# PEER expert gates: scattered into tables in DRAM and read back, in place of one-hot matmuls

## The chip, the cores and the metric

One Trainium2 chip; the kernel runs on one of its cores. The metric is device time in microseconds of one execution. Times of single executions are shown as median, lowest and highest; a profile is of one execution, whose own time is given beside it.

## The reference, cut to what matters

Two transformer layers for 256 tokens of width 2048 (a gated delta net with memory attention, then pooling and sparse attention), and at the end of the second an expert layer with 16384 experts, which the change touches:

```python
def peer_ffn(x, wq, sub_keys, u, v):          # per token, 8 heads
    qh = (xc @ wq).reshape(PEER_CHUNK, PEER_HEADS, 2, PEER_HALF)
    s1 = jnp.einsum('thd,kd->thk', qh[:, :, 0], sub_keys[0])
    s2 = jnp.einsum('thd,kd->thk', qh[:, :, 1], sub_keys[1])
    v1, i1 = lax.top_k(s1, PEER_TOPK)         # 16 of 128 first keys
    v2, i2 = lax.top_k(s2, PEER_TOPK)         # 16 of 128 second keys
    cand = v1[..., :, None] + v2[..., None, :]
    cidx = i1[..., :, None] * PEER_KEYS + i2[..., None, :]
    best, pos = lax.top_k(cand, PEER_TOPK)    # 16 of 256 pairs
    expert = jnp.take_along_axis(cidx, pos, axis=-1)
    gate = jax.nn.softmax(best, axis=-1)
    act = jax.nn.gelu(jnp.einsum('td,thkd->thk', xc, u[expert]))
    return jnp.einsum('thk,thkd->td', gate * act, v[expert])
```

An expert is a pair (i, j) of a first and a second key. Each token has 8 x 16 = 128 picks, and one expert may be picked by several heads: its gates then add.

## The kernel before

The kernel does not gather rows of u and v. It multiplies all 256 tokens with all 16384 rows of u, applies gelu, multiplies each of the 256 x 16384 results by its gate (zero for an expert that was not picked), and multiplies that by all rows of v. The results stand in `G`, a tile of 128 partitions (the second key j) x 128 rows (the first key i) x 256 tokens, 128 KB a partition.

All matrix products are made of three matmuls per tile in a rounded fp32 form (`fp32r`): weights and activations are split into a high part and a remainder. Class `Stream` (`ws`, L40 on) brings the weights of all matrices one after the other as granules of 512 KB: SP issues the load into a `wraw` tile, ACT copies the high part to `wh`, DVE subtracts it for the remainder `wl`. From w_q on there are three tiles of each. A granule of w_u feeds 24 matmuls, and w_u has 256 granules: two for each row i. `wstat` (L304) runs w_u by pairs of rows and calls `u_done` for each pair, which writes gelu of the sums into `G`. All multiplications, additions and copies below go through one helper, so most rows of the profile have its line, L123.

Side work is written as generators in a list `sides`. While PE's matmuls are emitted, `pump` steps the generators, and these hold back their next instruction until an estimated clock of their engine is near PE's (`after`, `on`, `spare`). So the program's order on each engine is fixed when it is built, and each engine's queue runs in that order.

The routing and the gates are such generators. `route()` (L1577 on) takes each head as the second half of w_q completes it: two small fp32 products per half of the tokens give the scores, DVE takes the best 16 of each side, of the 256 sums again 16, and after the last head picks the key numbers by comparisons (`eq`), softmaxes the gates and transposes both so that tokens lie along the free axis (`pickT`, `ghl`). Its scratch tiles lie in rows of `G` that w_u has not reached. `gate()` then walks over the tokens by two, 128 times:

```python
            for a in range(2):
                pe.matmul(out=ps[:, a * 256:a * 256 + 256], lhsT=oj[:, a, :],
                          rhs=og2[:, a].rearrange("p h i -> p (h i)"), start=True, stop=True)
            if t0:
                into(t0 - 2)
```

`oj` is the one-hot form of a token's 128 second keys (128 picks x 128 keys), `og2` that of its first keys times the gates, high part and remainder; the product is the token's 128 x 128 table of gates. DVE builds the one-hots (`oi`, `oj`), ACT scales them (`og2`, four instructions), and `into` adds the two parts and multiplies them into the rows of `G` that hold gelus already. `u_done` does the converse for tokens whose gates stand there.

After w_u, `split_h` splits the rows of `G` in turn for the product with w_v, into four tile pairs (`eog`, `eghl`, `eoj`, `ewg`). During w_v, `residual()` loads `hres` and `row` on POOL's queue and applies the last norm's terms on DVE.

Of the kernel before, what the change touches and what calls it, by code (L numbers as in the profile page):

```python
# [23 lines left out]
T = 256  # L24
# [14 lines left out]
class Stream:  # L39


    def __init__(self, nc, act, dve, pool, granules, raw_bufs, split_bufs):
        self.nc, self.act, self.dve, self.src = nc, act, dve, granules
        self.nl = self.ns = self.ng = 0
        self.raw, self.parts = {}, {}
        self.raw_slots = [(pool, f"wraw{n}") for n in range(raw_bufs)]
        self.split_slots = [(pool, f"{n}") for n in range(split_bufs)]
        self.extra, self.until = [], 0

# [13 lines left out]
    def _load(self):  # L63
        if self.nl < len(self.src):
# [6 lines left out]
            self.nl += 1  # L71

# [81 lines left out]
def tile_blocks(ctx, tc, P, out, dbg=None, stop=None):  # L154
# [1022 lines left out]
    cap[0] = 4  # L1177
    for k in range(2):
        split_y(16 + k, (yh[:, k, :], yl[:, k, :]))
    for c in range(4):  # L1180
        if c > 1:
            pts[c % 2] = [bank(), bank()]
            out_mm(c, 0, 16, hh, hl)
# [9 lines left out]
    if stop == "x1":  # L1193
        return

# [341 lines left out]
    pickT = rp.tile([128, 2, T], BF16, name="pickT")  # L1537
    iof = odd[:, :32].bitcast(U8)
    pool.iota(iof, pattern=[[1, 128]], base=0, channel_multiplier=0, allow_small_or_imprecise_dtypes=True)
# [21 lines left out]
    eq = carve(92, [128, 16])  # L1561
    idf = carve(90, [2, 8, 2, 16])
    pab = carve(88, [2, 2, 128])
    pk = carve(84, [2, 3, 128])
    sk = carve(83, [2, 128])
    act.dma_start(out=sk, in_=P["sk"])
    st4 = {"q": 0, "t0": 0, "ib": 0}
# [15 lines left out]
    def route():  # L1583
        for h in range(8):
# [12 lines left out]
            for t in range(2):  # L1597
# [5 lines left out]
                yield from spare("V", SV)  # L1603

        dve.tensor_copy(out=idf, in_=idxs)
        sm = odd[:, 32:].rearrange("p (t h) -> p t h", t=2)
        for t in range(2):
            tt(pk[:, t, 2, :].rearrange("p (h r) -> p h r", h=8), best[:, t], bc(best[:, t, :, 0:1], [128, 8, 16]), OP.subtract)
        act.activation(out=pk[:, :, 2, :], in_=pk[:, :, 2, :], func=AF.Exp)
        pf = pos.rearrange("p t h r -> p t (h r)")  # L1610
        ts(pab[:, 1].bitcast(U32), pf, 15, None, op0=OP.bitwise_and)
        ts(pf, pf, 4, None, op0=OP.logical_shift_right)
        dve.tensor_copy(out=pab[:, 0], in_=pf)
        yield
        dve.reduce_sum(out=sm, in_=pk[:, :, 2, :].rearrange("p t (h r) -> p t h r", h=8), axis=AX.X)
        dve.reciprocal(out=sm, in_=sm)
        dve.tensor_copy(out=pab[:, 1], in_=pab[:, 1].bitcast(U32))
        for t in range(2):
            g = pk[:, t, 2, :].rearrange("p (h r) -> p h r", h=8)
            tt(g, g, bc(sm[:, t, :, None], [128, 8, 16]), OP.mult)  # L1620
        yield
        eq4 = eq.rearrange("p (h r) a -> p h r a", h=8)
        for t in range(2):
            for f in range(2):
                tt(eq, bc(iof[:, None, :16], [128, 128, 16]), bc(pab[:, f, t, :, None], [128, 128, 16]), OP.is_equal)
                yield from spare("V", SV)
                tt(eq4, eq4, bc(idf[:, t, :, f, None, :], [128, 8, 16, 16]), OP.mult)
                yield from spare("V", SV)
                dve.reduce_sum(out=pk[:, t, f, :], in_=eq, axis=AX.X)
                yield from spare("V", SV)  # L1630
        for t in range(2):
            ps = yield from get()
            for j in range(3):
                pe.transpose(out=ps[:, j * 128:j * 128 + 128], in_=pk[:, t, j, :], identity=ident)
            yield
            sl = slice(t * 128, t * 128 + 128)
            copy_act(pickT[:, :, sl], ps[:, :256].rearrange("p (j t) -> p j t", j=2))
            copy_act(ghl[:, 0, sl], ps[:, 256:384])
            dve.follow("A")
            tt(ghl[:, 1, sl], ps[:, 256:384], ghl[:, 0, sl].bitcast(F32), OP.subtract)  # L1640
            put(ps)
        yield
        sides.append(gate())

    def gate():

        st4["on"] = True
        ohs, sums = {}, {}

        def one_hots(t0):  # L1650
            oi = rp.tile([128, 2, 128], BF16, name="oi", bufs=2)
            oj = rp.tile([128, 2, 128], F32R, name="oj", bufs=2)
            sl = slice(t0, t0 + 2)
            tt(oi, bc(iof[:, None, :], [128, 2, 128]), bc(pickT[:, 0, sl, None], [128, 2, 128]), OP.is_equal)
            tt(oj, bc(iof[:, None, :], [128, 2, 128]), bc(pickT[:, 1, sl, None], [128, 2, 128]), OP.is_equal)
            ohs[t0] = oi, oj

        def gated(t0):
            og2 = rp.tile([128, 2, 2, 128], F32R, name="og2")
            for a in range(2):  # L1660
                for p in range(2):
                    act.activation(out=og2[:, a, p, :], in_=ohs[t0][0][:, a, :], func=AF.Copy,
                                   scale=ghl[:, p, t0 + a:t0 + a + 1].bitcast(F32))
            ohs[t0] += (og2,)

        def into(t0):
            ps, w, wg = sums.pop(t0)
            ib = st4["ib"]
            sl = slice(t0, t0 + 2)
            if ib < 128:  # L1670
                tt(G[:, ib:, sl], wg[:, ib:], w[:, 1, ib:], OP.add)
            if ib:
                tt(wg[:, :ib], wg[:, :ib], w[:, 1, :ib], OP.add)
                tt(G[:, :ib, sl], G[:, :ib, sl], wg[:, :ib], OP.mult)
            put(ps)
            st4["t0"] = t0 + 2

        one_hots(0)
        one_hots(2)
        yield from on("V")  # L1680
        gated(0)
        ready = clk["A"], clk["V"]
        for t0 in range(0, T, 2):
            while clk["P"] < max(ready) - 0.4:
                yield
            t = clk["P"]
            ps = yield from get()
            _, oj, og2 = ohs.pop(t0)
            for a in range(2):
                pe.matmul(out=ps[:, a * 256:a * 256 + 256], lhsT=oj[:, a, :],  # L1690
                          rhs=og2[:, a].rearrange("p h i -> p (h i)"), start=True, stop=True)
            if t0:
                into(t0 - 2)
            yield from on()
            w = ps.rearrange("p (t h i) -> p h i t", t=2, h=2)
            wg = rp.tile([128, 128, 2], F32, name="wg", bufs=2)
            if t0 + 2 < T:
                gated(t0 + 2)
                ra = clk["A"]
            copy_act(wg, w[:, 0])  # L1700
            sums[t0] = ps, w, wg
            if t0 + 4 < T:
                one_hots(t0 + 4)
            ready = ra, clk["V"]
            while clk["P"] < t + TICK:
                yield
        into(T - 2)
        split_h(0)
        split_h(1)

    HS = {}
# [16 lines left out]
    def u_done(c0, m, pt):  # L1728
        t0 = st4["t0"]
# [267 lines left out]
```

## Time and profile before

| what | value |
|---|---|
| time, median of 3 runs | 2809.67 us (2805.61 to 2814.22) |
| the profiled execution's own time | 2811.53 us |
| its span, first to last instruction | 2809.8 us |
| granted clock of TensorE, mean | 0.996 |
| weights from DRAM | 490.27 MB on the first hardware queue |
| instructions of PE | 19455 matmuls |
| instructions of DVE, ACT, POOL | 3530, 2626, 595 |

Busy time of an engine is the time in which it executes; its share is over the whole span and averages over stages with different limits. PE is a busy engine here, so the table by stretch and the chain of waits say where something other than PE sets the pace.

### The profile page before, as it was taken

To read this page: it belongs to the slowest core of one execution; us is meant where nothing else is said; L and a number is where in the kernel's file an instruction comes from. 1 tells how busy PE (TensorE), PEld (TensorE's weight loads), DVE (VectorE), ACT (ScalarE), POOL (GpSimd) and SP (SyncE) were. 2 spreads that over 40 slices of the span, in tenths; PEclk is the share of its full clock that TensorE was granted. 3 is DMA by queue.
4 is the path that set the end of the run, shared out by engine and by line. 5 is a ranking of instruction groups with operands and counts; after the bars stand their busy time and mean duration, and the time that the engine had idled before them with its cause. 6 is when DMAs were issued, how large, how long until landed. Compare 5 with 4: busy or idle time off the path is not lost.

```text
span 2809.8 us, 50244 instructions
## 1 busy us (share of the span) xinstructions
PE 2774.0 (99%) x19455; PEld 2554.2 (91%) x19455; DVE 1907.1 (68%) x3530; ACT 1569.4 (56%) x2626; POOL 281.0 (10%) x595
## 2 busy tenths in 40 slices
PE   9999999999999999999999999999999999999998
PEld 7999999999888999879999999999998888888886
DVE  5746777775554655657998777778876655665555
ACT  7455666665544444444445777777765555445553
POOL 0001655654001000000000000000010000000000
PEclk9999999999999999999999999999999999999999
DMA  8636655555566666446666566666666766666664
GB/s 301 182 120 185 198 167 176 167 166 171 183 190 183 190 199 183 146 149 204 189 186 190 178 181 181 181 181 181 181 213 216 221 192 193 193 195 194 193 192 140
DMA packets 147839, 522.17 MB, mean 186 GB/s; under 512 B 18848, under 2 KB 20440, under 8 KB 147088
## 3 DMA queue, kind: packets, MB, share of 16 engines
q1 hardware_dynamic: 135504, 490.27, 57.6%
q0 software_dynamic: 8272, 19.43, 2.7%
q10 hardware_dynamic: 3824, 9.26, 0.9%
q8 instruction: 152, 2.49, 0.4%
q14 instruction: 87, 0.71, 0.1%
HBM read 512.84 MB, written 5.99 MB: 185 GB/s over the span
## 4 chain that ended last, share of the span: by engine, by line
PE 94%; DVE 2%; DMA 2%; ACT 1%; issue 1%; SPq 0%; POOL 0%; ACTq 0%; POOLq 0%; DVEq 0%
PE bank L123 94%; DMA wrawwraw<-in_w_v 1%; DVE wl L123 1%; ACT wh L123 0%; DVE hres L123 0%; DMA wrawx<-in_w_kv 0%; DMA wrawwraw<-in_w_q 0%; DVE small L123 0%; ACT y L123 0%; DMA G<-in_sk 0%; DMA hot<-in_bucket_hot 0%; ACT whx L123 0%; DVE sso L123 0%; DVE wlx L123 0%; DVE wko L123 0%
## 5 line engine op out<-in xcount | busy, mean ns | idle before, releaser
L123 DVE TENSOR_TENSOR wl<-wrawwraw,wh 128x1024 fp32r<-128x1024 f32 (+1 forms) x837 | 1020.4, 1224 | 688.5 <-ACT wh L123 686.4
L123 ACT ACTIVATE wh<-wrawwraw 128x1024 fp32r<-128x1024 f32 (+1 forms) x837 | 882.1, 1058 | 865.4 <-PE bank L123 732.2
L123 PE MATMUL bank<-hh,wh 128*128 128x256 f32 x3376 | 949.0, 281 | 1.1 <-ACT hh L123 1.1
L123 PE MATMUL bank<-hl,wh 128*128 128x256 f32 x3376 | 941.0, 279 | 0.4 <-DVE hl L123 0.2
L123 PE MATMUL bank<-hh,wl 128*128 128x256 f32 x3376 | 940.1, 278 | 0.0
L123 PEld LDWEIGHTS bank<-hh,wh 128*128 128x128 f32 x3376 | 638.3, 189 | 2.5 <-ACT hh L123 1.4
L123 PEld LDWEIGHTS bank<-hl,wh 128*128 128x128 f32 x3376 | 637.0, 189 | 1.3 <-DVE hl L123 0.9
L123 PEld LDWEIGHTS bank<-hh,wl 128*128 128x128 f32 x3376 | 634.8, 188 | 0.0
L123 ACT ACTIVATE og<-oi,ghl 128x128 fp32r<-128x128 bf16 x512 | 162.9, 390 | 25.7 <-PE bank L123 25.1
L123 DVE TENSOR_TENSOR wlx<-wrawx,whx 128x1024 fp32r<-128x1024 f32 x96 | 118.1, 1230 | 82.7 <-ACT whx L123 82.6
L123 ACT ACTIVATE whx<-wrawx 128x1024 fp32r<-128x1024 f32 x96 | 101.8, 1060 | 122.3 <-PE bank L123 112.5
L123 PE MATMUL bank<-wh,eghl 128*128 128x512 f32 x512 | 147.5, 389 | 0.6 <-ACT wh L123 0.6
L123 PE MATMUL bank<-wh,eog 128*128 128x512 f32 x512 | 147.4, 389 | 0.0
L123 PE MATMUL bank<-wh,ewg 128*128 128x512 f32 x512 | 147.4, 389 | 0.0
L123 PE MATMUL bank<-wh,eoj 128*128 128x512 f32 x512 | 147.4, 389 | 0.0
L123 PEld LDWEIGHTS bank<-wh,eghl 128*128 128x128 f32 x512 | 96.0, 188 | 20.9 <-ACT wh L123 1.0
L123 PEld LDWEIGHTS bank<-wh,eog 128*128 128x128 f32 x512 | 96.0, 188 | 20.3 <-ACT wh L123 0.4
L123 PEld LDWEIGHTS bank<-wh,ewg 128*128 128x128 f32 x512 | 96.2, 188 | 19.9
L123 PEld LDWEIGHTS bank<-wh,eoj 128*128 128x128 f32 x512 | 96.1, 188 | 19.8
L123 PE MATMUL bank<-gh,wh 128*128 128x256 f32 x392 | 110.6, 282 | 0.0
L123 PE MATMUL bank<-gl,wh 128*128 128x256 f32 x392 | 108.5, 277 | 0.0
L123 PE MATMUL bank<-gh,wl 128*128 128x256 f32 x392 | 108.4, 277 | 0.0
(394 smaller groups left out, 4540.4 us busy)
## 6 DMA issues: line engine op xcount, KB each, us to landing
wrawwraw<-in_w_u SPq DMA_DIRECT2D x256, 512.0 KB, 3.8
wrawwraw<-in_w_v SPq DMA_DIRECT2D x256, 512.0 KB, 4.3
wrawwraw<-in_w_dn SPq DMA_DIRECT2D x134, 512.0 KB, 4.3
wrawwraw<-in_w_out SPq DMA_DIRECT2D x73, 512.0 KB, 3.6
wrawwraw<-in_w_in SPq DMA_DIRECT2D x61, 512.0 KB, 4.2
wrawx<-in_w_dn SPq DMA_DIRECT2D x44, 512.0 KB, 3.7
wrawwraw<-in_w_q SPq DMA_DIRECT2D x32, 512.0 KB, 4.2
wrawwraw<-in_w_kv SPq DMA_DIRECT2D x23, 512.0 KB, 5.7
```

The lines of the kernel that those rows point to most:

```text
L123: return f(*a, **kw)
```

## The change

The gates of all experts are built in two tables in DRAM (`W_d`, one for each half of the tokens, [j, i, token], 8 MB each). The tables are filled with zeros by 64 transfers of 256 KB out of a tile that POOL clears; SP issues one behind each weight load, 32 in w_out and 32 in w_in2. `route()` computes picks and softmax per head (`gates_of`), adds up the gates of repeated picks by 32 DVE instructions that compare a pick's code with all picks so far and accumulate the products, and POOL writes each of the 16 x 2 columns of 128 sums to its 128 places by an indirect transfer, so the last write of a repeated pick has the full sum. `gating()` loads the tables by pairs of rows i, from w_u's row 92 on, and DVE multiplies `G` by them. `u_done` is only the gelu. The one-hot work, the transposes, and `gate()` go.

```diff
@@ class Stream
+        self.between, self.gap = iter(()), 0
@@ def _load
                 self.nc.sync.dma_start(out=t[:, sl], in_=self.src[self.nl][:, sl])
             self.raw[self.nl] = t
             self.nl += 1
+            self.gap -= 1
+            if self.gap < 0:
+                for o, i in self.between:
+                    self.nc.sync.dma_start(out=o, in_=i)
+                    break
@@ before w_out
+    W_d = [dram.tile([128, 128, 128], F32, name=f"W_d{t}") for t in range(2)]
+    zsrc = y_t[:, 24:, :].rearrange("p a t -> p (a t)")
+    zeros = [(W_d[t][:, 4 * n:4 * n + 4, :], zsrc[:, 512 * (n % 4):512 * (n % 4) + 512].rearrange("p (i t) -> p i t", t=128))
+             for t in range(2) for n in range(32)]
     for c in range(4):
+        if c == 1:
+            pool.memset(zsrc, 0.0)
+            ws.between = iter(zeros[:32])
+            ws.gap = 6
@@ before w_in2
+    ws.between = iter(zeros[32:])
+    ws.gap = 12
@@ route(), at the end of each head's top 16
+            yield from gates_of(h)
+        sides.append(gating())
+
+    def gates_of(h):
+        n = 16 * h
+        g = gate[:, :, n:n + 16]
+        tt(g, best[:, :, h, :], bc(best[:, :, h, 0:1], [128, 2, 16]), OP.subtract)
+        act.activation(out=g, in_=g, func=AF.Exp)
         for t in range(2):
...
+            tt(eq.rearrange("p (f r) a -> p f r a", f=2), bc(iof[:, None, None, :], [128, 2, 16, 16]),
+               bc(pab[:, :, :, None], [128, 2, 16, 16]), OP.is_equal)
+            tt(eq.rearrange("p (f r) a -> p f r a", f=2), eq.rearrange("p (f r) a -> p f r a", f=2),
+               bc(idf[:, :, None, :], [128, 2, 16, 16]), OP.mult)
+            dve.reduce_sum(out=pick.rearrange("p f r -> p (f r)"), in_=eq, axis=AX.X)
+            yield from spare("V", SV)
+            c = code[:, t, n:n + 16]
+            stt(c, pick[:, 1], 128.0, pick[:, 0], OP.mult, OP.add)
+            ts(put_at[:, t, n:n + 16], c, 128.0, tok, op0=OP.mult, op1=OP.add)
+        dve.reduce_sum(out=gsum[:, :, 0], in_=g, axis=AX.X)
+        dve.reciprocal(out=gsum, in_=gsum)
+        tt(g, g, bc(gsum, [128, 2, 16]), OP.mult)
+        yield from spare("V", SV)
+        for r in range(16):
+            for t in range(2):
+                k = slice(n + r, n + r + 1)
+                stt(junk[:, :n + 16], code[:, t, :n + 16], code[:, t, k], gate[:, t, :n + 16], OP.is_equal, OP.mult,
+                    accum=put_val[:, t, k])
+            yield from spare("V", SV)
+            for t in range(2):
+                pool.indirect_dma_start(out=W_d[t].rearrange("j i t -> (j i t)")[:, None],
+                                        out_offset=bass.IndirectOffsetOnAxis(ap=put_at[:, t, k], axis=0),
+                                        in_=put_val[:, t, k], in_offset=None)
+
+    def gating():
+        wts = {}
+        def load(b):
+            wt = rp.tile([128, 2, 2, 128], F32, name="wt", tag=WT[b // 2 % 3])
+            for t in range(2):
+                pool.dma_start(out=wt[:, t], in_=W_d[t][:, b:b + 2, :])
+            wts[b] = wt
+        while st4["ib"] < 92:
             yield
+        for b in range(0, 4, 2):
+            load(b)
+        yield from after(12)
+        for b in range(0, 128, 2):
+            if b + 4 < 128:
+                load(b + 4)
+            while st4["ib"] < b + 2:
                 yield
+            g = G[:, b:b + 2, :].rearrange("p b (h t) -> p b h t", h=2)
+            tt(g, g, wts.pop(b).rearrange("p h b t -> p b h t"), OP.mult)
+            yield from after(1.8)
+            yield from spare("V", 1.5)
         split_h(0)
         split_h(1)
+    WT = ("og2", "ghl", "wt")
...
     def u_done(c0, m, pt):
...
+        act.activation(out=G[:, c0:c0 + 2, :], in_=pt.rearrange("p (c t) -> p c t", c=2), func=AF.Gelu)
         st4["ib"] = c0 + 2
```

On POOL, behind the stores of the layer norm's result, the order before had one iota and then the loads of `hres` for w_v's stage:

```order
L123 DMA n_d_13152<-x1_9519 128x2048 [waits DMASW4_49,DVE_49,Activation_49]
L123 IOTA odd_76 128x128
L123 DMA hres_25591<-n_d_13152 128x512 [waits DVE_49,DMASW3_49,PE_49,DMASW5_49,Activation_49,Pool_49]
L123 DMA hres_25591<-n_d_13152 128x512 [waits DMASW6_49,DMASW4_49]
L123 DMA row0_25592<-in_ln1rows 128x512
```

The changed kernel has there, from its first scatters (names: `wt_14501` holds sums and addresses, `W_d0` and `W_d1` are the tables; DMASW is a transfer issued by POOL):

```order
L129 DMA W_d0_9527<-wt_14501 2097152x1 [waits DVE_49]
L129 DMA W_d1_9528<-wt_14501 2097152x1 [waits DVE_49]
L129 DMA W_d0_9527<-wt_14501 2097152x1 [waits DMASW5_49,DVE_49]
L129 DMA W_d1_9528<-wt_14501 2097152x1 [waits DMASW6_49,DVE_49]
L129 DMA W_d0_9527<-wt_14501 2097152x1 [waits DMASW7_49,DVE_49]
```

and from its last scatter to the loads of the tables:

```order
L129 DMA W_d1_9528<-wt_14501 2097152x1 [waits DMASW2_49,DVE_49]
L129 DMA wt_21650<-W_d0_9527 128x256 [waits DMASW3_49]
L129 DMA wt_21650<-W_d1_9528 128x256 [waits DMASW4_49]
L129 DMA wt_21653<-W_d0_9527 128x256
L129 DMA wt_21653<-W_d1_9528 128x256
L129 DMA wt_21802<-W_d0_9527 128x256
L129 DMA wt_21802<-W_d1_9528 128x256
L129 DMA wt_21836<-W_d0_9527 128x256 [waits DMASW6_49,DMASW5_49,DVE_49]
```

256 scatters and 128 loads have come in between the iota and the loads of `hres`; each scatter waits for the one before it to the same table, and the loads stand behind all scatters.

On DVE in w_u, the order before in the gate stretch (rows for two tokens: one-hots, splits, sums into `G`):

```order
L123 TENSOR_TENSOR oi_23562<-odd_76,pickT_14433 128x256
L123 TENSOR_TENSOR oj_23563<-odd_76,pickT_14433 128x256 [waits PE_49]
L123 TENSOR_TENSOR wl1_23569<-wrawwraw1_23463,wh1_23568 128x1024 [waits DMAHW3_49,PE_49,Activation_49]
L123 TENSOR_TENSOR wl2_23599<-wrawwraw2_23511,wh2_23598 128x1024 [waits DMAHW4_49,PE_49,Activation_49]
L123 TENSOR_TENSOR G_14422<-wg_23555,bank6_23543 128x24x2
L123 TENSOR_TENSOR wg_23555<-wg_23555,bank6_23543 128x208
L123 TENSOR_TENSOR G_14422<-G_14422,wg_23555 128x104x2 [waits DVE_49]
```

In the changed kernel the sums of repeated picks stand among the splits from the first granule of w_u on, eight between two of them; shown are those of the first head:

```order
L129 TENSOR_TENSOR wl2_14969<-wrawwraw2_14898,wh2_14968 128x1024 [waits DMAHW7_49,PE_49,Activation_49]
L129 SCALAR_TENSOR_TENSOR G_14489,wt_14501<-G_14489 128x16 [waits DVE_49] x8
L129 TENSOR_TENSOR wl0_15013<-wrawwraw0_14931,wh0_15012 128x1024 [waits DMAHW0_49,PE_49,Activation_49]
L129 SCALAR_TENSOR_TENSOR G_14489,wt_14501<-G_14489 128x16 [waits DVE_49] x8
L129 TENSOR_TENSOR wl1_15059<-wrawwraw1_14966,wh1_15058 128x1024 [waits DMAHW1_49,PE_49,Activation_49]
```

The multiplies by the loaded gates begin ahead of the split of granule 192 (counting from 0), one per granule:

```order
L129 TENSOR_TENSOR wl2_21787<-wrawwraw2_21722,wh2_21786 128x1024 [waits DMAHW7_49,PE_49,Activation_49]
L129 TENSOR_TENSOR G_14489<-G_14489,wt_21650 128x512 [waits DMASW6_49,DMASW5_49]
L129 TENSOR_TENSOR wl0_21821<-wrawwraw0_21753,wh0_21820 128x1024 [waits DMAHW0_49,PE_49,Activation_49]
L129 TENSOR_TENSOR G_14489<-G_14489,wt_21653 128x512 [waits DMASW7_49,DMASW0_49]
L129 TENSOR_TENSOR wl1_21855<-wrawwraw1_21784,wh1_21854 128x1024 [waits DMAHW1_49,PE_49,Activation_49]
```

DVE's work on gates has moved: the sums stand in the first half of w_u, the multiplies in its last quarter, each with the next split behind it. A multiply waits for its two loads.

On ACT at the end of w_u, the splits of `G`'s first rows stood ahead of the last gelus (`gt` from a bank):

```order
L123 ACTIVATE eog2_25539<-G_14422 128x256 [waits DVE_49,Activation_49]
L123 ACTIVATE eghl_25542<-G_14422 128x256
L123 ACTIVATE wh2_25553<-wrawwraw2_25474 128x1024 [waits DMAHW1_49,PE_49]
L123 ACTIVATE gt_25581<-bank7_25422 128x256 [waits PE_49]
L123 ACTIVATE gt_25584<-bank7_25422 128x256 [waits DVE_49]
```

Now they stand behind the last gelu, and wait for DVE's last multiply:

```order
L129 ACTIVATE wh2_24047<-wrawwraw2_23985 128x1024 [waits DMAHW1_49,DVE_49,PE_49]
L129 ACTIVATE G_14489<-bank0_23952 128x512 [waits PE_49]
L129 ACTIVATE eog2_24077<-G_14489 128x256 [waits DMASW4_49,DMASW3_49,DMASW5_49,DMASW2_49,DMASW6_49,DMASW1_49,DMASW7_49,DMASW0_49,DVE_49]
L129 ACTIVATE eghl_24080<-G_14489 128x256 [waits DMASW2_49,DMASW7_49,DMASW1_49,DMASW0_49]
```

The last pair of rows has moved to the head of the chain into w_v.

## Rows read from the trace of the kernel before

**Rows 1.** The page: busy us, share of the span, instructions.
```profile
PE 2774.0 (99%) x19455; PEld 2554.2 (91%) x19455; DVE 1907.1 (68%) x3530; ACT 1569.4 (56%) x2626; POOL 281.0 (10%) x595
```

**Rows 2.** Chain of waits, 1300 to 2078: start and length in us.
```profile
1300.77 236.09 PE bank L123 x2073
1537.85 1.27 ACT og L123 x4
1539.17 538.73 PE bank L123 x4648
```

**Rows 3.** Busy time of each engine by stretch; the first row names the columns.
```profile
core 0: us, PE busy (x) PEld busy (x) DVE busy (x) ACT busy (x) POOL busy (x), PEclk, DMA share, GB/s
1303.00:1322.00 19.00, 19.00 (x163) 19.00 (x162) 15.97 (x49) 7.43 (x7) 0.00 (x0) 1.00 0.53 160
1325.00:1475.00 150.00, 150.00 (x1326) 150.00 (x1325) 140.56 (x416) 70.07 (x78) 0.00 (x0) 1.00 0.61 187
1450.00:1529.00 79.00, 79.00 (x699) 79.00 (x699) 73.34 (x102) 37.31 (x40) 0.00 (x0) 1.00 0.65 194
2095.00:2120.00 25.00, 23.31 (x99) 18.07 (x98) 12.46 (x17) 12.30 (x18) 4.30 (x8) 1.00 0.90 329
```

**Rows 4.** Groups of instructions, gates: busy us, mean ns, idle before.
```profile
L123 PE MATMUL bank<-og,oj 128*128 128x256 f32 x256 | 51.0, 279 | 0.1
L123 DVE TENSOR_TENSOR oj<-odd,pickT 128x256 fp32r<-128x256 uint8 x128 | 53.6, 418 | 0.0
```

**Rows 5.** Groups of instructions, those like the end of w_u.
```profile
L123 ACT ACTIVATE G<-bank 128x512 f32<-128x512 f32 x33 | 18.6, 588 | 3.6 <-PE bank L123 3.6
L123 DVE TENSOR_TENSOR hres<-hres,row 128x512 f32<-128x512 f32 x24 | 16.1, 689 | 0.9 <-ACT hres L123 0.6
L123 ACT ACTIVATE eog<-G 128x256 fp32r<-128x256 f32 x64 | 25.6, 399 | 2.7 <-DVE G L123 2.7
```

**Rows 6.** Groups of instructions, DVE's routing and the nearest to the sums.
```profile
L123 DVE TENSOR_TENSOR wl<-wrawwraw,wh 128x1024 fp32r<-128x1024 f32 (+1 forms) x837 | 1020.4, 1224 | 688.5 <-ACT wh L123 686.4
L123 DVE MAX8 G<-G 128x8 f32<-128x128 f32 (+1 forms) x96 | 32.3, 336 | 2.2
L123 DVE FIND_INDEX8 G<-G 128x8 uint32<-128x128 f32 (+1 forms) x96 | 31.7, 330 | 0.0
L123 DVE MATCH_REPLACE8 G<-G 128x128 f32<-128x128 f32 (+1 forms) x48 | 15.4, 321 | 0.0
L123 DVE MATCH_VALUE_LOAD G<-G 128x8 f32 x144 | 12.3, 86 | 3.3
L123 DVE SCALAR_TENSOR_TENSOR junk<-bank,ident 128x128 f32<-128x128 f32 x24 | 7.0, 291 | 13.1 <-PE bank L123 12.7
L123 DVE DVE_READ_ACCUMULATOR junk<-bank,ident 128x1 f32 x24 | 2.0, 83 | 0.0
L123 DVE SCALAR_TENSOR_TENSOR sm_sk<-sm_wk,sm_sk 128x2 f32<-128x2 f32 x36 | 5.8, 162 | 1.2
```

**Rows 7.** DMA issues: KB each, median us from issue to landing.
```profile
Lb<-scr_l POOLq DMA_DIRECT2D x24, 128.0 KB, 4.7
row<-in_ln2rows POOLq DMA_DIRECT2D x8, 256.0 KB, 5.9
hres<-n_d POOLq DMA_DIRECT2D x8, 256.0 KB, 8.3
scr_x<-Xs POOLq DMA_DIRECT2D x24, 32.0 KB, 2.2
```

**Rows 8.** POOL's waits: us in total, times, longest us.
```profile
POOL Lb L123 <- DMA scr_l<-lq: 15.6, 5, 3.8
POOL Xg L123 <- DMA scr_x<-Xs: 14.8, 5, 3.9
```

**Rows 9.** One tile each on POOL: shortest/median/longest ns, when.
```profile
L123 POOL DMA_DIRECT2D scr_l<-lq x48: 551/551/622, 239.1 to 634.1; - x48
L123 POOL TENSOR_TENSOR itmp<-Lb,Xs x186: 208/298/1350, 289.2 to 673.4; 128x60 f32<-128x60 f32 x18, 128x28 f32<-128x28 f32 x12, 128x54 f32<-128x54 f32 x12, 128x48 f32<-128x48 f32 x12
```

More of the change, by code (lines that the diff above doesn't have):

```diff
@@ L1536, in tile_blocks @@
     rp.tile([128, 24], F32, name="gap")
-    pickT = rp.tile([128, 2, T], BF16, name="pickT")
-    iof = odd[:, :32].bitcast(U8)
-    pool.iota(iof, pattern=[[1, 128]], base=0, channel_multiplier=0, allow_small_or_imprecise_dtypes=True)
+    small = rp.tile([128, 64], F32, name="small")
+    wt0 = rp.tile([128, 2, 2, 128], F32, name="wt")
+    put_at = wt0[:, 0].rearrange("p a t -> p (a t)").rearrange("p (t k) -> p t k", t=2).bitcast(U32)
+    put_val = wt0[:, 1].rearrange("p a t -> p (a t)").rearrange("p (t k) -> p t k", t=2)
     def carve(b0, shape, dt=F32):
@@ L1560, in tile_blocks @@
     wrk = carve(100, [256])
[L1561 to L1564, printed above, removed]
+    eq = carve(98, [32, 16])
+    idf = carve(96, [2, 16])
+    pab = carve(95, [2, 16])
+    pick = carve(94, [2, 16])
+    gsum = carve(93, [2, 1])
+    code = carve(92, [2, 128])
+    gate = carve(91, [2, 128])
+    junk = carve(90, [128])
+    iof = carve(89, [16])
+    tok = carve(88, [1])
+    pool.iota(iof, pattern=[[1, 16]], base=0, channel_multiplier=0, allow_small_or_imprecise_dtypes=True)
+    pool.iota(tok, pattern=[[0, 1]], base=0, channel_multiplier=1, allow_small_or_imprecise_dtypes=True)
     sk = carve(83, [2, 128])
     act.dma_start(out=sk, in_=P["sk"])
-    st4 = {"q": 0, "t0": 0, "ib": 0}
+    st4 = {"q": 0, "ib": 0, "put": 0}
     def q_done(c0, m, pt):
@@ L1603, in route @@
                 yield from spare("V", SV)
-        dve.tensor_copy(out=idf, in_=idxs)
-        sm = odd[:, 32:].rearrange("p (t h) -> p t h", t=2)
-        for t in range(2):
[L1608 to L1634, printed above, removed]
-            yield
[L1636 to L1684, printed above, removed]
-                yield
[L1686 to L1707, printed above, removed]
@@ L1728, in u_done @@
     def u_done(c0, m, pt):
-        t0 = st4["t0"]
-        assert c0 < 82 or "on" in st4
-        pv = pt.rearrange("p (c t) -> p c t", c=2)
-        g = G[:, c0:c0 + 2, :]
-        if t0 == 0:
-            act.activation(out=g, in_=pv, func=AF.Gelu)
-        else:
-            for c in range(2):
-                gt = rp.tile([128, T], F32, name="gt")
-                act.activation(out=gt, in_=pv[:, c, :], func=AF.Gelu)
-                tt(g[:, c, :t0], g[:, c, :t0], gt[:, :t0], OP.mult)
-                if t0 < T:
-                    dve.tensor_copy(out=g[:, c, t0:], in_=gt[:, t0:])
+        act.activation(out=G[:, c0:c0 + 2, :], in_=pt.rearrange("p (c t) -> p c t", c=2), func=AF.Gelu)
         st4["ib"] = c0 + 2
@@ L1756, in tile_blocks @@
     row = [vp.tile([128, D], F32, name=f"row{n}") for n in range(2)]
-    small = rp.tile([128, 64], F32, name="small", tag="pickT")
     bst2 = small[:, :48].rearrange("p (m c s) -> p m c s", m=2, c=4)
@@ L1760, in tile_blocks @@
     rs2, wk2, nm2 = (small[:, n:n + 2].rearrange("p (m s) -> p m s", s=1) for n in (52, 54, 56))
-    dg = rp.tile([128, 2, 128], F32, name="dg", tag="gt")
+    dg = rp.tile([128, 2, 128], F32, name="dg", tag="wt")
     st5 = {"res": False}
```

7 lines of the change are left out of this document (added).

## The prediction, made before the changed kernel ran

> **What bounds the kernel now.** I read the page first: its list of engines says whether one engine fills the span. TensorE does, 2774.0 of 2809.8 us, 99% [rows 1]. So a change pays only where it takes work off PE or makes PE's own instructions pass faster, and it costs wherever PE has to wait. Next the chain of waits, to see whether the stretch that the change touches has gaps. From 1300.77 to 2077.90 us it is PE and nothing else, but for 1.27 us in which ACT builds the first gate operand: 236 us with the last half of w_q and the routing, then 538.73 us in which 4648 matmuls pass, the 256 gate ones among them [rows 2]. Third, the table of busy time by stretch, because two things decide the price: the pace of PE with and without the gate matmuls, and how much room DVE has beside them [rows 3]. In 1325 to 1475 PE is busy 150.00 of 150.00 us, while DVE is busy 140.56. PE does not wait there although DVE has 6% left.
>
> **Gate matmuls, and the pace of the others: -42.3 us.** The group has 256 matmuls of 128x256, and the row's mean of 279 ns is no price, since matmuls overlap [rows 4]. The price is pace. In the gate stretch 538.73 us / 4648 = 115.9 ns each [rows 2]. Where no small matmul stands between the wide ones, 699 pass in 79 us, 113.0 ns [rows 3]. The change leaves 4648 - 256 = 4392 matmuls there. At 113.0 ns they take 496.4 us: 42.3 us less. Of it 256 x 115.9 ns = 29.7 is the removed work, and 12.7 the better pace of the rest. The bound on the other side is the pace of 1303 to 1322, 163 in 19 us or 116.6 ns, also without gate matmuls: 512.1 us, only 26.6 less. I take the fast end, for 1450 to 1529 is the same w_u loop. Six transposes of the old routing go too: 6 x 0.116 = 0.7 us.
>
> **The end of w_u: +2.2 us.** Before, the splits of G's first rows stand ahead of the last gelus on ACT. Now the last pair of rows needs gelu, then the multiply by its loaded gates, then the split, and the first matmuls of w_v wait for that split's place behind the gelu. PE's last matmul 0.3 us, gelu 588 ns (a 128x512 ACT row out of a bank), multiply 689 ns (the 128x512 DVE row), split 399 ns [rows 5], and hops of some 0.2 make 2.2. Before there is no such gap.
>
> **DVE while it routes: +8 us (0 to 20).** A head's place is 17.7 granules of w_u, on PE 17.7 x 24 x 0.113 + 0.9 (the head's own products) = 48.9 us. DVE owes in it: 17.7 wl subtractions x 1.224 = 21.7; the top 16, of which all eight heads' rows add to 32.3 + 31.7 + 15.4 + 12.3 = 91.7, with the sixteen sums of candidates 16 x 0.418 (priced by the 128x256 oj row) = 6.7, together 12.3 a head; the picks, for two halves of the tokens 2 x 0.69 + 0.69 + 7 x 0.16 = 3.2 each, 6.4; softmax 0.7; and 32 sums of repeated picks. No row has these. The nearest are the same operation at 128x2 (162 ns) and at 128x128 (291 ns), and the widths run from 16 to 128, so 0.23, and 83 ns to read the accumulator (taken from the row of the same name): 0.31 x 32 = 9.9 [rows 4, 6]. The sum is 51.0 against 48.9: 2.1 short a head, 17 over eight, if nothing overlaps. Before, at 94% busy, PE did not feel DVE at all [rows 3]; and the three split slots let it run ahead. I take 8. What it is on: the wl subtractions are queued behind those sums, and PE waits for wl. ACT loses 512 operations and the gelus become one 128x512 each; it has room in every window, so I cost that at nothing.
>
> **Zero fills and loads: +2 us (0 to 10).** 64 transfers of 256 KB on SP's queue stand among the weight loads of w_out and w_in2, one behind a load of 512 KB: half as much again for the engines. The stream runs at about 190 GB/s, so some 290 in those stretches. The fullest window of before has 329 GB/s at a share of 0.90, and there PE was busy 23.31 of 25 us, with the loads of hres and row on POOL beside the stream [rows 3]. So up to 2 us is likely. In the gating 256 KB more come every granule (2.71 us), 96 GB/s, the same 290. A load has three buffers, so some 7 us to land; the rows say 4.7 us (128 KB), 5.9 and 8.3 (256 KB) [rows 7]. That is near the edge, hence 10. The DVE multiplies of the gating (689 ns beside 1224 per granule of 2712) are covered by DVE's slack there.
>
> Sum against the profiled execution's 2811.5: -42.3 - 0.7 + 2.2 + 8 + 2 = -30.8, so 2780.7. That execution lies 1.9 above the median of the runs shown, which makes 2779; I write **2780**.
>
> **The scatters: at nothing, if a pair takes under 4.2 us.** 256 transfers of 128 single floats, from POOL. The order shows that each waits for the one before it to the same table, and that the loads stand behind all of them on POOL. Let a pair (one to each table) take P. The first can go at about 1339: w_u starts at 1300.8 + 384 x 0.113 + 1.8 = 1346 and DVE is some 2.5 granules ahead. The first multiply stands ahead of granule 192's wl, so DVE comes to it at about 1346 + 189.5 x 2.71 + 15 = 1874. Less 5 for the load, and with 3 of slack, the last scatter must have landed at 1872. So 533 us for 128 pairs: 4.16 us. Over that, time grows by 128 us for each us of P: DVE waits in the multiply with the next wl behind it, and PE runs dry. The gain is gone at P = 4.4.
> What is P? No indirect transfer is in the trace. The nearest are POOL's small writes to DRAM with another POOL instruction behind them that needs them landed: Lb waits 15.6 us in 5 times for scr_l and Xg 14.8 in 5 for scr_x, 3.0 to 3.1, at most 3.9 [rows 8]; with one issue of 0.55 to 0.6 a step of 3.6 to 3.7, at most 4.5. Both tables' steps overlap but for one more issue. Reading 128 addresses is unknown: nothing, or as much as another issue (0.6). I take 3.9, the scr_l step and part of that; the ends are 3.3 (2.2 us to land [rows 7], two issues) and 5.1. At 3.9 the last lands at 1838 and nobody waits.
> A rule speaks against that. POOL's issues are short beside a busy DVE: 551 ns, 622 at most, while POOL's own subtraction from SBUF spreads from 208 to 1350 ns [rows 9]. The Trainium skill, "SBUF — State Buffer", section "SBUF: two separate sides", says that DVE and GpSimd share a port pair under an exclusive lock, so that a transfer issued by POOL can stand still while DVE holds it, about 3.1 us in place of 0.62. By its figure a pair would be an estimate of 6.2 us or more and the time about 3040; the direct issues of this trace show no such stretch.
>
> **Rivals.** (A) The scatters come late. For it: 3.9 is 6% from the turn, the longest wait would already be past it, and an issue that reads its addresses from SBUF may stretch as itmp does. Against it: the mean step is below. A1, plain cost: P = 4.2 to 4.7 gives 2781 + 128 x (P - 4.16), 2786 to 2850. A2, the issue stretched by DVE's work (the mechanism of the rule above): 0.6 to 1.2 us more per pair, P = 4.5 to 5.1, 2824 to 2901. This is the side of slower; it decides from P = 4.4 on. (B) DVE becomes the bound while routing: each of the 256 sums 0.1 us dearer is 26 us, with the 8 above, and the gain is gone: 2797 to 2811. For it: 94% busy already. Against it: the rows of the same operation lie close together. (C) The pace stays slow without gate matmuls: 15.7 us of the gain missing, about 2796; within my own range.
>
> **How the numbers follow.** Forecast, scatters in time (C with it): 0.45, with 2766 to 2800 as its own range (no DVE stall and no contention make 2769, less 3 for the spread of the runs). A1 0.25, A2 0.15, B 0.15. What a measurement here can tell from no change is 0.3%, 8.4 us: 2801 to 2818. Faster: 0.45, and 0.05 each of A (P under 4.3) and B: 0.55. Same: 0.04 of A, 0.06 of B: 0.10. Slower: 0.31 of A and 0.04 of B: 0.35. The range goes from 2766 to 2890 (P = 5.0): some 0.05 lie under it and 0.1 over it.
>
> **What would show it.** Right: about 113 ns per matmul from 1350 to the end of w_u, the last scatter landed before 1872, no wait of DVE for a wt load, a gap of about 2 us at the start of w_v. Wrong: PE idle behind wl from about 1875 on, with DVE's multiply waiting for wt (A; P can be read as the spacing of scatters to one table, and A2 as their time of issue); or PE idle behind wl in 1350 to 1740 (B); or 116 to 117 ns a matmul (C). Most at risk is P, since the trace has no scatter.

## The result, and the profile after

| what | before | changed |
|---|---|---|
| time, median of 4 runs | 2807.66 us (2805.61 to 2814.22) | 2843.69 us (2842.9 to 2847.16) |
| ratio, 95% interval | | 1.0127 (1.0107 to 1.0147) |
| the profiled execution, its span | 2811.53, 2809.8 us | 2843.1, 2841.4 us |
| granted clock of TensorE, mean | 0.996 | 0.982 |

The change is slower by 1.3%. The forecast of 2780 us was wrong, in size and in sign; rival A, the late scatters, is what happened.

The page of the changed kernel (busy us, share of the span, instructions):

```profile
PE 2732.4 (96%) x19193; PEld 2511.5 (88%) x19193; DVE 1828.4 (64%) x3447; ACT 1402.1 (49%) x1955; POOL 656.2 (23%) x981
```

Against [rows 1], PE has lost 41.6 us of work, and yet the span is 31.6 us longer: some 73 us of PE's time are idle that were not. What PE waited for (us in total, times, longest us):

```profile
PE bank L129 <- DVE wl L129: 76.9, 5, 74.3
PE bank L129 <- ACT wh L129: 5.0, 1, 5.0
...
PE bank L129 <- ACT eog L129: 1.9, 1, 1.9
```

One wait of 74.3 us for a `wl`. The same list for DVE says why that `wl` was late: DVE stood in a multiply of `G` until its loaded gates came, once, for 78.5 us.

```profile
DVE G L129 <- DMA wt<-W_d: 78.5, 1, 78.5
1944.06 0.69 DVE L129 TENSOR_TENSOR G<-G,wt 128x512 f32<-128x512 f32 x1 [78.54 <-DMA wt<-W_d]
```

The second line is that multiply in the timeline: DVE stood at it from 1865.5, and PE ran dry 6.1 us later, at 1871.7.

The chain of waits, from inside w_u (start us, length us), leads from there to the scatters; it answers to [rows 2]:

```profile
1551.30 284.67 PE bank L129 x2509
1837.10 1.24 DVE wl L129
1840.30 4.66 DMA W_d<-wt
...
1939.15 2.14 DMA W_d<-wt
1942.14 2.36 DMA wt<-W_d
1944.67 1.23 DVE wl L129
1945.94 176.28 PE bank L129 x1534
```

So the last scatter was issued at 1939.15 and landed 2.14 us later, the first load took 2.36 us, and PE went on at 1945.94. The list by tile gives the 256 scatters (shortest, median, longest ns of the issue; first and last start), and the loads behind them:

```profile
L129 POOL DMA_INDIRECT W_d<-wt x256: 967/972/2021, 1334.2 to 1939.2; - x128
L129 POOL DMA_DIRECT2D wt<-W_d x128: 536/538/581, 1940.3 to 2106.8; - x128
```

From 1334.2 to 1939.2 are 605 us for 127 pairs: P is 4.76 us, not 3.9. Up to the stall it was more. The 161st scatter starts at 1737.68, 80 pairs behind the first: 5.04 us each. The timeline of POOL shows how the scatters come there, and how in the stall (start, length, idle before):

```profile
1740.04 1.21 POOL L129 DMA_INDIRECT W_d<-wt  x1 [1.39 <-issue]
1742.88 1.09 POOL L129 DMA_INDIRECT W_d<-wt  x1 [1.63 <-DMA W_d<-wt]
1744.89 1.80 POOL L129 DMA_INDIRECT W_d<-wt  x1 [0.92 <-DMA W_d<-wt]
...
1905.13 0.97 POOL L129 DMA_INDIRECT W_d<-wt  x1 [0.63 <-issue]
1906.41 0.97 POOL L129 DMA_INDIRECT W_d<-wt  x1 [0.31 <-issue]
1908.02 0.97 POOL L129 DMA_INDIRECT W_d<-wt  x1 [0.64 <-issue]
```

In the stall, with the other engines and the weight stream at rest, a pair takes 1908.02 - 1905.13 = 2.9 us (3.07 as the mean of the last head). The table of busy time by stretch shows that rest (columns as in [rows 3]):

```profile
1720.00:1860.00 140.00, 140.00 (x1238) 140.00 (x1237) 63.64 (x52) 60.58 (x65) 71.53 (x52) 1.00 0.67 195
1873.00:1939.00 66.00, 0.00 (x0) 0.00 (x0) 0.00 (x0) 0.00 (x0) 42.72 (x44) 0.52 0.02 1
1946.00:1951.00 5.00, 5.00 (x25) 5.00 (x26) 3.97 (x5) 0.25 (x1) 2.99 (x7) 0.55 0.86 265
1950.00:2000.00 50.00, 50.00 (x441) 50.00 (x441) 32.88 (x36) 21.33 (x23) 19.22 (x36) 1.00 0.92 297
2000.00:2060.00 60.00, 60.00 (x532) 60.00 (x531) 40.20 (x44) 26.43 (x29) 23.48 (x44) 1.00 0.91 291
```

The stall cost PE a little more than its 74.3 us: in the first 5 us of work behind it, at a granted clock of 0.55, 25 matmuls passed, where 44 pass at 113.1 ns. That is 2.1 us more, 76.4 in all. The rows also show what went as forecast: 1238 matmuls in 140 us are 113.1 ns each, and in 2000 to 2060, with the table loads beside the stream (291 GB/s at a share of 0.91), PE is busy 60 of 60 us.

Where the time went, read from the starts of ACT's copy of the same granule in the two profiled executions (changed less before, us; w_u has granules 0 to 255):

```
first of w_q             -5.1
w_u, granule   0         -7.4
w_u, granule 128        -16.1
w_u, granule 190        -29.4
w_u, granule 204        +43.9      (the stall lies between)
w_u, granule 252        +32.8
w_v, granule  12        +34.7
w_v, granule 250        +33.6
```

Ahead of w_q the code differs only by the zero fills; the 5 us there come and go between executions (other kernels below have +2 to -7), so they are no effect of the change. Without the 76.4 us of the stall the changed kernel would have had some 2767 us.

### The profile page after: what moved, and what is told of

The parts are those of the page before. It is cut to its first block, busy times and chain, and to the rows that moved or that the text cites. A ratio compares the mean times of both kernels' runs of the same rounds, so it can differ in the third digit from the quotient of the medians.

```text
span 2841.4 us, 49582 instructions
## 1 busy us (share of the span) xinstructions
PE 2732.4 (96%) x19193; PEld 2511.5 (88%) x19193; DVE 1828.4 (64%) x3447; ACT 1402.1 (49%) x1955; POOL 656.2 (23%) x981
## 4 chain that ended last, share of the span: by engine, by line
PE 87%; DVE 6%; DMA 3%; issue 2%; POOL 1%; ACT 1%; ACTq 0%; SPq 0%; DVEq 0%; POOLq 0%
PE bank L129 87%; DVE G L129 2%; DVE wl L129 2%; POOL W_d L129 1%; DMA W_d<-wt 1%; DMA wrawwraw<-in_w_v 1%; ACT wh L129 0%; DMA wrawwraw<-in_w_kv 0%; DMA wrawwraw<-in_w_out 0%; DVE small L129 0%; DVE hres L129 0%; DMA wrawwraw<-in_w_q 0%; ACT y L129 0%; DMA hot<-in_bucket_hot 0%; DVE sso L129 0%
## 5 line engine op out<-in xcount | busy, mean ns | idle before, releaser
L129 PE MATMUL bank<-hh,wl 128*128 128x256 f32 x3376 | 936.4, 277 | 76.4 <-DVE wl L129 76.4
L129 POOL DMA_INDIRECT W_d<-wt x256 | 306.0, 1195 | 347.5 <-DVE G L129 184.2
L129 POOL TENSOR_TENSOR hres<-hres,row 128x512 f32<-128x512 f32 x4 | 5.8, 1476 | 576.1 <-DVE hres L129 576.1
```

Of the source, the lines that this page charges most:

```text
L129: return f(*a, **kw)
```

## Experiments

Each ran once with a profile, beside the kernel before on the same chip (2808.14 us in the first four that were run, 2807.72 as the median of 7 in the next four, 2804.84 in the last three); v1_two_tables ran four times. Three theories of the long pairs are put against each other. Theory 1: a scatter waits for the landing of the one before it, and landings are slow behind the weight stream. Theory 2: DVE's operations hold up POOL's issues. Theory 3: handling the addresses costs.

**Four tables for each half of the tokens**

```diff
+    W_x = [[W_d[t]] + [dram.tile([128, 128, 128], F32, name=f"W_x{t}{n}") for n in range(3)] for t in range(2)]
-                pool.indirect_dma_start(out=W_d[t].rearrange(...)[:, None],
+                pool.indirect_dma_start(out=W_x[t][r % 4].rearrange(...)[:, None],
```

> Scatters go round four tables for each half of the tokens, so that one waits for the fourth before it and not for the last; only the first table of each half is read, so three quarters of the gates are left out. Theory 1 (landing chain): nothing waits for a landing, a pair takes its two issues, 2.4 us and some, or the 3.1 us in which DVE delivers the sums; the last scatter starts by about 1740 and PE has no stall: 2768 (2762 to 2776). Theories 2 and 3 (POOL's own time per scatter): pairs stay above 4.2 us, the stall is at least half of the 74 us, 2800 or more.

Measured: 2775.99 us. The scatters by tile, and PE's wait:

```profile
L129 POOL DMA_INDIRECT W_d<-wt x64: 964/972/1929, 1340.2 to 1725.8; - x64
```
```profile
L129 POOL DMA_INDIRECT W_x<-wt x192: 965/976/2013, 1342.9 to 1734.0; - x192
```
```profile
PE bank L129 <- DVE wl L129: 6.1, 10, 1.4
```

With the chain loosened, a pair takes (1734.0 - 1340.2) / 127 = 3.1 us, about what DVE needs to deliver the sums, and the stall is gone. The issues are as long as before and DVE does the same work, so neither of these alone can make 5.0. The wait for the landing is the cause of the stall.

**Plain writes, without and with the chain**

```diff
-                pool.indirect_dma_start(...)
+                pool.dma_start(out=W_d[t][:, n + r, 0:1], in_=put_val[:, t, k])     # e1_direct
+                pool.dma_start(out=W_d[t][:, 0, 0:1], in_=put_val[:, t, k])         # e5_plain_chain
```

> The 256 scatters become plain writes of the same 128 floats each, one to a place per partition that is known when the program is built, with the same two chains; the gates so end up in the wrong places. Theory 1 (each write waits until the one before it to the same table has landed, and landing is slow behind the weight stream): the pairs still come every 4.2 to 4.8 us, 0.2 to 0.9 less than the 5.0 to 5.4 of the scatters, and PE still stalls 0 to 65 us: 2768 to 2835. Theory 2 (POOL's issue is stretched by DVE's operations, since it reads addresses from SBUF): issues of 0.55 to 0.62 us that no DVE operation stretches, and a pair near 4.3. Theory 3 (handling addresses is what costs): pairs under 3.6 us, no stall, 2768.

> As e1_direct, but each of the plain writes goes to the same place of its table, so that it has to wait for the one before it to the same table; in e1_direct the places differed, and the program had no such wait. The gates are left out of their places. Theory 1 (waiting for the landing is the price, whatever the form of the write): pairs of 3.8 to 4.8 us, the last near 1830 to 1935. Theory 3 (handling addresses is what costs): pairs of 2.5 us or less, one landing less the addresses, the last before 1720.

Measured: 2771.93 and 2769.79 us.

```profile
L129 POOL DMA_DIRECT2D W_d<-wt x256: 537/537/547, 1334.5 to 1708.7; - x128
```
```profile
L129 POOL DMA_DIRECT2D W_d<-wt x256: 537/537/550, 1337.0 to 1834.9; - x128
```

The first of the two was no test of the chain, and its expectation was wrong on that. Its writes go to places that the program knows to differ, so none waits for another, and each head's 16 pairs follow DVE's sums. It shows two things by the way: a plain write's issue is 0.54 us whatever DVE runs, and DVE delivers the sums in time (the last write is at 1708.7). The second has the chain: (1834.9 - 1337.0) / 127 = 3.92 us a pair, in theory 1's span. That is the price of a plain chained write beside the stream, and it is to two digits the value that the prediction took for the scatters. A scatter costs 1.1 more beside the same stream (5.04).

**Less of the weight stream**

```diff
+            if self.one[0] <= self.nl < self.one[1] and (self.nl - self.one[0]) % 2:   # e4_half_stream
+                t = self.last
...
+            if self.one[0] + 3 <= self.nl < self.one[1]:                               # e6_no_stream
+                t = self.kept[self.nl % 3]
```

(`one` holds the first granule of w_u and of w_v; for these granules the load is left out.)

> In w_u only every second granule is loaded and used twice, so the weight stream is halved while ACT, DVE and PE do the same; half of the products of w_u are so computed with the wrong weights. Theory 1 (landing behind the stream): landing falls from 4.7 us to about 3.5, the pairs from 5.0 to 5.4 to about 4.0, the last scatter is at about 1850 and PE's stall under 15 us: 2768 to 2783. Theory 2 (DVE's operations): pairs stay at 4.8 or more, stall 65 to 75 us, 2835 to 2845.

> In w_u only the first three granules are loaded and used again and again, so that the weight stream is gone while ACT, DVE and PE do the same work; nearly all of w_u's products are with the wrong weights. The half stream took the pairs from 5.0 to 5.4 to 4.3 to 5.1. Theory 1 with the stream as the cause of slow landings: pairs of 3.1 to 3.6 us in the routing, the last scatter before 1800, no stall, 2766 to 2778. If DVE's work is the other half of the cause: pairs of 3.9 to 4.4, the last at 1835 to 1900, stall up to 30 us.

Measured: 2817.56 and 2766.66 us.

```profile
L134 POOL DMA_INDIRECT W_d<-wt x256: 964/972/2016, 1339.9 to 1914.4; - x128
PE bank L134 <- DVE wl L134: 40.8, 3, 40.3
```
```profile
L135 POOL DMA_INDIRECT W_d<-wt x256: 963/972/2007, 1333.9 to 1776.8; - x128
```

The scatters' median landing in the changed kernel, and with half the stream (us, the last number; the traces show the landing of 32 and of 96 of the 256):

```profile
W_d<-wt POOLq DMA_INDIRECT x256, 4.0
W_d<-wt POOLq DMA_INDIRECT x256, 3.2
```

So the landing does fall with the stream (the 4.7 in the expectation had the zero fills in it), but the time was outside both theories: pairs of 4.5 us, a last scatter at 1914 and a stall of 40 us. Theory 1 had forecast too much; a stream of half the bytes in the same large granules still slows the pairs by 1.0 us over none. Without the stream a pair takes (1776.8 - 1333.9) / 127 = 3.49 us, while DVE and ACT work on, and the stall is gone. The stream costs 5.04 - 3.49 = 1.55 us a pair.

**wl by another operation, and by another engine**

```diff
-   dve.tensor_tensor(out=l[:, sl], in0=r[:, sl], in1=h[:, sl].bitcast(F32), op=OP.subtract)
+   dve.tensor_scalar(out=l[:, sl], in0=r[:, sl], scalar1=1e-4, scalar2=None, op0=OP.mult)    # e3_wl_one_input, w_u only
...
+   act.activation(out=l[:, sl], in_=r[:, sl], func=AF.Copy, scale=1e-4)                      # e7_wl_on_act, w_u only
```

> In w_u, DVE makes wl from the raw weight alone (times a constant), an operation with one input from SBUF in place of two; the low part of the weights of w_u is so left out. Theory 2 (the issue is stretched by DVE operations that read two inputs): issues that start while wl runs take 0.97 us as the others, mean 0.97 to 1.0 in place of 1.2, and the pair falls from 5.1 by at least 0.5 us; if the lock also delays the descriptors, by over 1 us, and the stall is gone (2768). Theory 1: the pair falls by 0.4 at most, since landing is what is waited for; stall 40 to 65 us, 2810 to 2835.

> In w_u ACT makes wl (a scaled copy of the raw weight), so that DVE has only the routing and the gating; the low part of the weights of w_u is left out. If DVE's operations cause half of the slow step: issues of 0.97 us, pairs of 4.0 to 4.4, nearer 4.0 behind the routing, the last before 1900 and a stall under 35 us. If they cause only the 0.23 us by which an issue is longer: pairs of 4.5 to 5.0 and a stall of 50 to 70 us. If ACT, now busy 2.1 of 2.7 us per granule, falls behind, the whole of w_u is longer by a few us.

Measured: 2838.85 and 2794.32 us.

```profile
L133 POOL DMA_INDIRECT W_d<-wt x256: 963/970/1475, 1340.8 to 1935.3; - x128
PE bank L133 <- DVE wl L133: 66.1, 2, 65.9
```
```profile
L133 POOL DMA_INDIRECT W_d<-wt x256: 963/967/1421, 1333.0 to 1939.5; - x128
PE bank L133 <- ACT eog L133: 24.1, 1, 24.1
```

The operation with one input takes 0.70 us in place of 1.22, and issues that start beside it are still stretched, now to 1.475 us at most; that theory 2 would be rid of the stretch with one input fell. Over the first 80 the pairs take 5.01 us, and the stall of 65.9 us and the time lie just past what theory 1 allowed. With wl on ACT hardly any issue is stretched. But the pairs are then still 4.78 us (4.71 over the first 80), and the last scatter is where it was. So DVE's wl costs 5.04 - 4.71 = 0.3 us a pair, no more. That e7's stall is only 24.1 us has another reason: no wl is queued on DVE behind the waiting multiply, so PE runs to the end of w_u before it waits (for `eog`, at 2051). A stall under 35 us had been forecast for the case that DVE's operations cause half of the slow step; it came, but not for that reason. The pair of 4.78 us is that of the other case.

**Nothing beside the chain**

> e6_no_stream and e7_wl_on_act in one: in w_u no weight stream and no wl on DVE; w_u's products are so with the wrong weights. With the stream gone a pair took 3.4 to 3.6 us, in the stall with stream and DVE at rest 3.07. If what is left, 0.4, is DVE's wl operations holding up the issues: pairs of 3.05 to 3.2, issues of 0.97 to 1.0, the last scatter near 1730. If not: 3.4 as before. No stall in either case; 2766 to 2775, if ACT keeps up.

> e5_plain_chain and e6_no_stream in one: plain writes to one place per table, and no weight stream in w_u; gates and weights of w_u are so wrong. A plain write's landing by itself: pairs of 2.2 to 2.9 us against 3.4 to 3.6 of the scatters without a stream, and 3.9 of plain writes beside it. If the addresses cost the same in both settings, 1.0 to 1.2 less than the scatters: 2.3 to 2.5. DVE delivers the sums at 3.06 a pair, so in the later heads it may be that one that shows. 2764 to 2772.

(The edits are those of the two kernels that each names.) Measured: 2779.46 and 2768.66 us.

```profile
L138 POOL DMA_INDIRECT W_d<-wt x256: 967/971/1403, 1339.3 to 1747.2; - x128
```
```profile
L135 POOL DMA_DIRECT2D W_d<-wt x256: 537/540/550, 1339.1 to 1722.8; - x128
```

Scatters: 407.9 / 127 = 3.21 us, the 0.3 less than without a stream alone that wl had cost beside it too. The time lies 4 us over its forecast: with wl on ACT, PE waited 8.9 us for `wh` (5.6 in the kernel before) and 3.8 for `wl`. Plain writes: 2.4 to 2.6 within a head (in the first, 1339.1 to 1378.0, 2.6), with pauses between heads for DVE. Together (5.04 is over the first 80 pairs, 2.5 within the heads, the others over all 127):

```
us per pair              beside the stream    without it
scatter                        5.04              3.49
scatter, wl not on DVE         4.78              3.21
plain write                    3.92              2.5
```

The plain writes differ from the scatters in one thing more: all of a table go to the same 128 places, where the scatters spread. How much of the step between them is the addresses and how much the places was not separated.

**The same kernel, gating begun later**

```diff
-        while st4["ib"] < 92:
+        while st4["ib"] < 104:
```

> The changed kernel with the loads and multiplies begun at w_u's row 104 in place of 92, 24 granules or 65 us later, and everything else as it is. If the stall is only the scatters' lateness: the last scatter again near 1939, PE's stall at the first multiply 74 - 65 = about 10 us. 21 pairs of rows are then left when w_u's matmuls end; at 1.4 to 2.0 us each (three buffers of loads) PE waits another 30 to 42 us there. Sum 2844 - 65 + 30 to 42 = 2808 to 2821. If the scatters were slowed by something at the fixed place of the first multiply, the stall would stay over 50 us.

Measured: 2835.89 us, dearer than expected. PE's waits:

```profile
PE bank L129 <- DVE wl L129: 36.5, 6, 33.7
PE bank L129 <- ACT eog L129: 31.2, 1, 31.2
```

The stall fell from 74.3 to 33.7 and not to 10, since the last scatter moved too, from 1939 to 1967. In the changed kernel the stall itself had quickened the last scatters: it stops the stream that they wait behind. A rule of so many microseconds of lateness per microsecond of P holds only up to the stall.

**A version made for the cause**

```diff
+    W_d = [[dram.tile([128, 128, 128], F32, name=f"W_d{t}{c}") for c in range(2)] for t in range(2)]
...
+                stt(junk[:, :n // 2 + 8], code[:, t, r % 2:n + 16:2], code[:, t, k], gate[:, t, r % 2:n + 16:2], OP.is_equal, OP.mult,
+                    accum=put_val[:, t, k])
...
+                pool.indirect_dma_start(out=W_d[t][r % 2].rearrange("j i t -> (j i t)")[:, None], ...)
...
+        while st4["ib"] < 70:
...
+            tt(w[:, 0], w[:, 0], w[:, 1], OP.add)
+            tt(g, g, w[:, 0], OP.mult)
```

> A version made for the cause found: each half of the tokens has two tables, for even and odd picks, so that a scatter waits for the one two pairs back; sums of repeated picks run within a table (half as wide), and DVE adds the two tables' rows before it multiplies (64 more operations of that size in all), from granule 148 on, 1.2 pieces of half a pair of rows per granule; 128 zero fills in place of 64, from a zeroed DRAM tile. Theory 1 (chain of landings): pairs of 2.6 to 3.2 us, last scatter before 1750, no stall at the first multiply, 2766 to 2785. Theories 2 and 3 (POOL's own time or DVE): pairs of 4 or more, a stall of over 100 us since the multiplies begin earlier, 2870 or more. Its own risk: the loads take 1.2 x 256 KB per granule, and PE loses up to 10 us to late granules.

Measured: 2778.29 us, median of 4 runs (2771.93 to 2780.15), against 2807.72 of the kernel before (7 runs): ratio 0.9894 (0.9872 to 0.9915).

```profile
L129 POOL DMA_INDIRECT W_d<-wt x256: 963/972/2013, 1333.5 to 1716.0; - x128
```
```profile
PE bank L129 <- DVE wl L129: 7.7, 9, 2.9
PE bank L129 <- ACT wh L129: 5.3, 2, 4.7
```

Pairs of 3.0 us, the last 150 us ahead of the time at which the changed kernel's DVE came to its first multiply, and no stall: 1.1% faster than before, 2.3% faster than the change (2778.29 / 2843.69). Its loads cost a little: one wait of 2.9 us for a wl at 1989, in a stretch at 285 to 303 GB/s.

## Why the prediction was wrong

**The step that failed** is "What is P? ... I take 3.9, the scr_l step and part of that". P was 5.04 us as long as the stream ran, 4.76 over all, and the turn stood at 4.16. The chain of waits per table and the turn were right: the first scatter came at 1334.2 (forecast 1339), DVE stood at the first multiply from 1865.5 (forecast 1874) and PE ran dry at 1871.7. By the 4.65 us from the last landing (1941.29) to PE's return (1945.94), the last scatter had until 1867.0, and (1867.0 - 1334.2) / 128 is again 4.16: the differences cancel. The rows that P was read from [rows 7, 8, 9] were plain writes, and a plain chained write beside the stream costs 3.92; that this is the 3.9 of the prediction is chance, for the rows by themselves gave 3.6 to 3.7. The runs put two things in its place. An indirect issue is longer, 0.97 against 0.54 us (the prediction had 0.6 a pair as the most for the addresses, taken in part), and with wl off DVE a pair of scatters costs 0.7 to 0.9 more than a pair of plain writes, in both columns of the table. And DVE's wl adds 0.3. Both were named as unknown, and the upper end of 5.1 held them; the likeliest value was put at the wrong end.

**Rival A.** Its formula, 2781 + 128 x (4.76 - 4.16), gives 2858; measured 2843.7. The difference lies in the base, some 2767 without the stall and not 2781; with it the formula gives 2844. That it then fits so well is in part luck, for P is the mean of pairs before the stall and of quicker ones in it. A1 and A2 were put as alternatives. They add up: of the 0.9 by which 5.04 exceeds the turn, 0.3 is A2's.

**The rule on the port pair** showed its form, not its figure. In the timeline a wl runs beside a scatter's issue:

```profile
1744.62 1.23 DVE L129 TENSOR_TENSOR wl<-wrawwraw,wh 128x1024 fp32r<-128x1024 f32 x1 [1.49 <-ACT wh L129]
```

It ends at 1745.85; the issue that began inside it, at 1744.89, ends at 1746.69, 0.84 later. Of the 256 issues, 120 start inside a wl, and 106 of these end 0.84 to 0.85 us after it; 68 start beside no DVE instruction and take 0.97 on average. That agrees with the Trainium skill, "SBUF — State Buffer", section "SBUF: two separate sides": whoever holds the pair keeps it for its whole instruction, then the other goes on. Its 3.1 us, which it gives for a transfer beside a copy on DVE, was not seen: the longest issue is 2.02 us, and a wl is 1.22 us long. By that figure the prediction had some 3040 us. Plain writes are not stretched beside the same wl (0.537 to 0.550).

**Gate matmuls and the pace: -42.3, and DVE while it routes: +8.** From granule 0 to 252, without the 76.4 us of the stall, the changed kernel gained 36.2 us; the two terms together said 34.3. By parts, the routing was cheaper and the gating dearer than forecast: from granule 0 to 128 the gain is 8.7 us where the removed gates, at 42.3 / 539 us of the stretch behind 1539, would give 13.3, so routing cost 4.6; behind 128 it is 27.5 against 29.0. In e5_plain_chain, which has no stall, the whole is 37.3. PE waited for wl 2.6 us in all besides the stall, so rival B did not come. The sums took about what was forecast (mean ns, busy us; then two of them and the read of the first in the timeline):

```profile
L129 DVE SCALAR_TENSOR_TENSOR G<-G 128x16 f32<-128x16 f32 (+7 forms) x272 | 78.0, 287 | 7.6
...
L129 DVE DVE_READ_ACCUMULATOR G<-G 128x1 f32 x256 | 21.2, 83 | 0.0
```
```profile
1699.71 0.35 DVE L129 SCALAR_TENSOR_TENSOR G<-G 128x128 f32<-128x128 f32 x1
1699.98 0.08 DVE L129 DVE_READ_ACCUMULATOR G<-G 128x1 f32 x1
1700.10 0.35 DVE L129 SCALAR_TENSOR_TENSOR G<-G 128x128 f32<-128x128 f32 x1
```

The operation is longer than taken, 0.29 against 0.23 us, but of the 83 ns of the read 75 lie within its end, and were not to be added. From one sum to the next it is 0.34 us on average, where 0.31 was taken: 0.9 us more a head, 7 over eight. That routing still cost only 4.6 fits the remark in the prediction that its sum holds if nothing overlaps.

**The end of w_u: +2.2.** PE waits 1.9 us for `eog`; right.

**Zero fills and loads: +2.** From the first of w_out to that of w_q the changed kernel lost 1.1 us (6.2 ahead, then 5.1). The table loads beside the stream cost nothing that PE shows. At 1.2 times the loads per granule, in v1_two_tables, they begin to cost. The term was right in size.

**Chances.** A had 0.40 against 0.45, and the time lies well inside the range of 2766 to 2890. The sign was decided by a number that the trace of before did not hold, with the turn inside its bounds; the likeliest case there is close to even.

## What to carry to other kernels

Where small writes to one table follow each other under a dependence, price the chain by landing, not by bandwidth or issue time, and take the landing from rows beside the same stream; then ask whether the writes need one table. A second table per half, with 128 adds of 0.42 us on an engine that has room, loosened the chain from 5.0 to 3.0 us a pair and turned +1.3% into -1.1%. When a deadline far down an engine's queue depends on such a chain, put the wait where nothing is queued behind it: with wl off that queue the same lateness cost 24 us in place of 74.

## What the runs showed of the hardware that was not expected

An indirect scatter of 128 floats takes POOL 0.97 us to issue, against 0.54 for a plain write of the same floats. A chained pair of scatters takes 3.07 us in the stall, with the other engines and the stream at rest, and 3.21 beside PE's and ACT's work without the stream and wl. A small write's median landing (us, the last number), without the stream in e9_plain_quiet and beside 512 KB granules at about 195 GB/s in e5_plain_chain:

```profile
W_d<-wt POOLq DMA_DIRECT2D x256, 0.5 KB, 1.7
W_d<-wt POOLq DMA_DIRECT2D x256, 0.5 KB, 3.4
```

Half of that stream takes back only a third of what it adds to a pair of scatters. At which point of the way to DRAM the write is held up was not tested. A DVE operation with an accumulator hides most of the read of the accumulator in its own end (75 of 83 ns). TensorE's granted clock was 0.52 of full in 1873 to 1939, when PE had nothing to do, and still 0.55 in 1946 to 1951, when PE was busy again; 0.5 is the lower of its two levels, 1.2 of 2.4 GHz. In the row from 1950 on it was full.
